# Four PSUM banks in turn for five products by token block, and modulation pieces only in the MLP's second products

## The chip, the cores and the metric

The kernel runs on one core of one Trainium2 chip. The metric is the device time of one launch in microseconds (us). The kernel before takes 2113.64 us, the median of three runs (2110.22 to 2122.06).

The engines are TensorE (PE; PEld is its loading of weights), VectorE (DVE), ScalarE (ACT), GpSimd (POOL) and SyncE (SP), which only issues DMAs here. Each of them works through its own list of instructions in order. PSUM, where PE leaves its products, has eight banks of 128 x 512 floats; DVE and ACT read them and so set them free ("evacuate").

## The reference

512 tokens of 1024 channels, batch 1, go through two blocks, all in float32. The first block has two attention layers, the second a convolution layer and a gated recurrence (hgrn), each of these two followed by an MLP of 4096 hidden channels. A vector `c` per block gives scale, shift and gate of each layer (the "modulation": `silu(c)` times a matrix). What the change touches:

```python
# even mixer: z = h @ w_in, split into
EVEN_SPLITS = [384, 256, 32, 512, 128, 128, 1024]   # cq, ckv, kr, sq, sk, sv, gate
k_rope = apply_rope(z_kr, cos_r, sin_r)             # 32 channels of a token
c_kv = rmsnorm(z_ckv, kv_norm)                      # kv = c_kv @ w_ukv
q = (rmsnorm(z_cq, q_norm) @ w_uq)                  # rope on 32 of each head's 96
q_s = apply_rope(z_sq, cos_h, sin_h)                # sliding window attention
# odd mixer: z = h @ w_in, its first three parts of 512 channels
q, k = apply_rope(z_dq, ...), apply_rope(z_dk, ...)
v_d = z_dv
# MLP of the second block
y = square(relu(h @ w1)) @ w2;  x = x + gate * y    # gate, and the next layer's scale, shift: silu(c) @ ada_w + ada_b
```

## The kernel before

A product in float32 is made of three products of split numbers (a high and a low part, "hTh" and "hTl" for the activations, `hl` for the weights), by `mm3` at L207. Activations stand channel-major, 8 chunks of 128 channels; tokens stand in four blocks of 128. `gemm_x` (`gemm_xs`, L287) computes one product by token block: for each of four blocks it asks for a PSUM bank, issues 24 matmuls (8 chunks x 3 terms) into it, and calls the product's evacuation `evac(tb, ps)`. Weights come in granules of 1024 columns: SP fetches `raw` (4 buffers), ACT casts it to the high part (L221), DVE or POOL makes the low part (L224); `hl` has 5 buffers.

The banks of PSUM are named by tag, `{"mm": 2, "sc": 2, "tp": 2, "pv": 1, "tq": 1}`. A `gemm_x` without `subs` takes the tag `mm`, so its token blocks use two banks in turn; one with `subs` (two parts per block) takes `mm` and `sc` by turns.

In the even mixer these stand one after the other: the product `cq` (L741), the library call `partition_broadcast` on POOL that spreads `nsink` (L745), the product `ckv` of 288 columns (L756; its evacuation takes a sum of squares on ACT, L553, the root on POOL, L386 and L388, a scaling on ACT, L751, and the rope), and the product `sq` of 512 columns (L777; evacuation by rope and a DMA). Then come 20 transposes of the latents (L784, evacuated by ACT, L202, and DVE, L203), the products `uq` and `ukv`, and the gates (L668). `rope` (L575 to L585) reads PSUM twice on DVE (L582 into the scratch tile `ru`, which has one buffer, and L584) and adds on POOL (L585), which sets `ru` free. In the odd mixer three products of 512 columns follow each other: `dq` and `dk` with rope and a DMA issued on ACT (L908), and `dv`, copied by ACT (L938). Before them `nlam` is spread by POOL (L928).

The modulation's vectors are queued (`ada`, L484) in steps: 8 per vector, each fetching 512 KB (`araw`) and adding two scaled rows on DVE (L502 first, then L504) to `acc`, which has one buffer; each fourth step ends a half vector with four small matmuls (L511, PSUM bank `tq` here) and additions (L513, L517). `group()` counts the groups of products (`ng`), and at every `tick_every`-th count `tick()` takes one step from the queue.

The MLP (`mlp`) goes by quarters q = 0 to 3 of its hidden channels. The first product of a quarter is two calls of `gemm_q`, a product of 512 channels in seven parts (L1186, banks `mm`, `sc`, `tp` in turn, sums on DVE at L1179); for q = 0 the first of the two is `gemm_wh` in plain form. `evq` squares the relu and splits it into `hid` (L199 on ACT, L200 on DVE). The second product is two calls of `gemm_x`, whose evacuation (L1100 on DVE, L1103 on POOL) adds to the resident x. Before the MLP of the convolution layer three vectors (24 steps) are queued; with `tick_every` at 2 they came out two per `gemm_q`, two per `gemm_wh` and two per `gemm_x` until the queue was empty.

The instructions of each engine are not in the order of the program: the scheduler takes each instruction with a priority by its place in the program and builds the engines' lists from an estimate of when each would be ready.

Of the kernel before, what the change touches and what calls it, by code (L numbers as in the profile page):

```python
# [26 lines left out]
# layout of the constant array  # L27
# [49 lines left out]
def constants():  # L77
# [16 lines left out]
    # of a row's block of 32: the columns of each level; of a row's block of 128: the block of 32 on the diagonal  # L94
# [13 lines left out]
def cap4(v, o):  # L108
    """512 elements of a DRAM vector as four rows of 128, each on 32 partitions"""
    return bass.AP(tensor=v.tensor, offset=v.offset + o, ap=[[P, 4], [0, 32], [1, P]])  # L110


class K:
# [33 lines left out]
    def scope(self, **bufs):  # L147
        """a pool of working tiles; bufs by tag"""
        @contextmanager
        def f():  # L150
            with self.tc.tile_pool(name=self.nm("wk"), bufs=1, reuse_waits="tile") as p:
                old = (getattr(self, "t4", None), getattr(self, "bufs", None))
                self.t4, self.bufs = p, bufs
                yield p
                self.t4, self.bufs = old
        return f()
# [18 lines left out]
    def oT_tiles(self, t0):  # L175
        """a mixer's output as a split pair: the first token block in t0, the others in the places of the activations
        that the mixer read"""
# [31 lines left out]
    def wgran(self, w, k0, nk, c0, cw, own=False):  # L209
        """weights rows [k0*128, (k0+nk)*128), cols [c0, c0+cw) -> split pair [128, 2, nk, cw]"""  # L210
# [16 lines left out]
    def wload(self, w, c0, cw, kc, own=0):  # L227
        """the weights of kc chunks of channels, the last granules in own tiles of the scope"""
# [9 lines left out]
    def rank(self, off):  # L238
        """instructions that the scheduler takes off places later than their place in the program"""
# [5 lines left out]
    def mark(self):  # L245
        """what comes from the queue of the modulation stays behind the work of DVE so far"""
# [6 lines left out]
    def advance(self, g, have, want):  # L253
        """steps of g until their cost reaches want; the cost so far"""
# [7 lines left out]
    def weave(self, main, n, fill, cost):  # L262
        """n steps of main, with fill of that cost (or of cost(i) after i steps) spread over them, and kept behind
        them on TensorE"""
# [22 lines left out]
    def gemm_xs(self, act, w, c0, cw, kc, evac, tag="mm", subs=None):  # L287
        """out[tok, c0:c0+cw] by token block; evac(tb, psums)"""
        gs = self.wload(w, c0, cw, kc)
        subs = subs or [(0, cw)]  # L290
        for tb in range(NTB):
            outs = []
            for s0, sw in subs:
                ps = self.psum(("mm", "sc")[tb % 2] if len(subs) > 1 else tag)
# [11 lines left out]
    def gemm_xk(self, act, gs, cw, kc, evac):  # L306
        """as gemm_x, with the channels outermost"""
# [9 lines left out]
    def gemm_tb(self, act, w, evac, after=None, late=None):  # L317
        """out[tok, 0:1024], a token block's two halves one after the other; evac(tb, half, psum). with late,
        the last channels come late: the first half of two token blocks does the others first, the second block after
        that instruction"""  # L320
# [29 lines left out]
    def gemm_ws(self, act, w, c0, cw, kc, evac, tag="mm"):  # L350
        """out[c0:c0+cw, tok] by chunks of 128 channels; evac(chunk, psum)"""
# [14 lines left out]
    def gemm_wh(self, act, jobs):  # L366
        """as gemm_w for jobs (w, c0, evac) of 256 channels, the first half of the tokens before the second"""
# [14 lines left out]
    def rstd(self, ss, n, cols=1):  # L382
        """(ss/n + eps)^-1/2"""
# [8 lines left out]
    def cond(self, cs):  # L392
        """silu of each vector of cs, as columns [128, 8]"""
# [10 lines left out]
    def start(self, x_in, c, c2, w, b, g, wg, cw):  # L404
        """norm and modulation of the first layer: the normalised x channel-major while the modulation's weights
        come in; returns silu(c) and the step that makes chunk k of the split pair"""
# [77 lines left out]
    def ada(self, ccol, w, b, c0, kind, g=None):  # L484
        """one vector of the modulation as a row in DRAM, queued in eight steps"""
# [50 lines left out]
    def group(self):  # L536
        """after each group of products of a weight"""
# [18 lines left out]
    def prenorm(self, act, tb, x, S, B, eng=None):  # L556
        """rmsnorm and modulation of token block tb [128 tok, 1024], to its columns of the split channel-major pair"""
# [15 lines left out]
    def rope(self, out, src, tb, nh, dim, co, so):  # L573
        """out, src [128, nh, dim] views; src in PSUM or SBUF"""
# [13 lines left out]
    def softmax(self, ps, n, mask, sink=None, norm=True):  # L588
        """ps holds minus the scores; returns the probabilities [128, n]"""
# [19 lines left out]
    def heads_T(self, src, n, sel, scale=None, tag="b4"):  # L609
        """src [128 tok, NTB, x]; sel(src, tb) -> [128, n]; transposed, split pair tile [128, 2, 512]"""  # L610
# [10 lines left out]
    def p_T(self, p, nb):  # L621
        """p [128 q, nb*128 keys] -> [128 keys, nb, 128 q]"""
# [8 lines left out]
    def pv32(self, out, V, p, qb):  # L631
        """out[:, qb] = sum over the key blocks V of V^T p^T, in float32"""
# [6 lines left out]
    def pv_pair(self, out, Vs, ps, qb):  # L639
        """the same for two heads of 64 channels, on the two halves of the columns of the array"""  # L640
# [8 lines left out]
    def pv_out(self, o, pv):  # L649
        """o = pv * o / 2, o holding twice the silu of the gate"""  # L650
# [11 lines left out]
    def gates(self, act, w, c0, o, cs):  # L662
        """o[c] = 2 silu(gate), with silu(x) = x (1 + tanh(x/2)) / 2"""
# [7 lines left out]
    def vec_cols(self):  # L671
        """per-channel vectors as columns: [128, 54]"""
# [20 lines left out]
    def out_first(self, o, w, xsrc, xdst, GG, S, B):  # L693
        """o: [128, 8, 512] fp32; returns the next split activations"""
# [1093 lines left out]
```

## Time and profile before

| what | value |
|---|---|
| median of three runs | 2113.64 us |
| span of the profiled execution | 2106.4 us |
| PE busy | 1943.9 us, 92% of the span |
| DVE busy | 1402.8 us, 67% |
| ACT busy, POOL busy | 884.5 us, 805.1 us |
| TensorE's mean granted clock | 0.959 of full |

The profile is of one execution, and its span runs from its first to its last instruction; the median of the runs is 7.2 us above it. The rows further below come from the page of that execution and from its trace. Times are from the start of the span. In a row of the timeline the first number is the start and the second the length in us (of xN instructions together), and the bracket at the end is how long the engine had waited and what ended the wait.

### The profile page before, as it was taken

What the parts mean: (1) busy time and instruction counts of PE and PEld (TensorE: products, weight loads), DVE (VectorE), ACT (ScalarE), POOL (GpSimd) and SP (SyncE); (2) the same over time, 40 slices, a digit from 0 to 9 for tenths busy, and PEclk for the clock granted to TensorE, in tenths of its full rate; (3) what the DMA queues carried; (4) which work ended last, traced back from release to release, by engine and by line L of the source; (5) the groups of instructions that cost most, each with busy time, mean ns of one, the idle gap of its engine ahead of it and who ended that gap; (6) DMA issues with size and microseconds to landing.
All of it is one profiled execution on the core that took longest, in us unless ns stands there. A gap on an engine that the chain in (4) does not pass through costs nothing.

```text
span 2106.4 us, 32096 instructions
## 1 busy us (share of the span) xinstructions
PE 1943.9 (92%) x12471; PEld 1580.0 (75%) x12471; DVE 1402.8 (67%) x1987; ACT 884.5 (42%) x1499; POOL 805.1 (38%) x701
## 2 busy tenths in 40 slices
PE   7799999897999988679899999999999998999998
PEld 5688667664776776448788989876777778898896
DVE  5356775545555769976987648667787858485673
ACT  4245553134544434333525436243454534352452
POOL 1223334222233448615232422455585544223232
PEclk9899979998999999889999999999999999999999
DMA  8384555366343751432554235453322322242331
GB/s 317 121 230 142 173 165 157 88 156 144 87 129 94 250 165 56 110 105 91 170 187 132 83 99 178 132 151 106 101 78 87 116 86 80 90 131 71 121 101 60
DMA packets 225024, 270.67 MB, mean 128 GB/s; under 512 B 26602, under 2 KB 145609, under 8 KB 224872
## 3 DMA queue, kind: packets, MB, share of 16 engines
q1 hardware_dynamic: 188982, 232.83, 36.3%
q10 hardware_dynamic: 35890, 35.79, 5.5%
q8 instruction: 98, 1.61, 0.3%
q14 instruction: 54, 0.44, 0.1%
HBM read 252.46 MB, written 16.12 MB: 128 GB/s over the span
## 4 chain that ended last, share of the span: by engine, by line
PE 49%; DVE 14%; issue 6%; DMA 6%; POOL 4%; ACT 2%; ACTq 0%; POOLq 0%; DVEq 0%; SPq 0%
PE mm L207 28%; PE sc L207 5%; PE mm L1186 4%; PE sc L1186 3%; PE tp L1186 3%; DVE acc L504 3%; DMA araw<-in_ada_w_dram 2%; DVE hl L224 2%; DVE ol L1312 2%; DVE hl L200 1%; DMA raw<-in_od_w_in_dram 1%; DVE X L1547 1%; PE pv L207 1%; DMA raw<-in_ada_w_dram 1%; PE tp L626 1%
## 5 line engine op out<-in xcount | busy, mean ns | idle before, releaser
L207 PE MATMUL mm<-hTh,hl 128*128 128x512 f32 (+1 forms) x1296 | 410.9, 393 | 19.0 <-ACT t L1339 7.0
L207 PE MATMUL mm<-hl,hid 128*128 128x512 f32 x1344 | 317.0, 395 | 5.3 <-DVE hid L200 3.8
L221 ACT CAST hl<-raw 128x1024 fp32r<-128x1024 f32 (+2 forms) x219 | 224.1, 1033 | 223.8 <-PE mm L207 133.8
L207 PEld LDWEIGHTS mm<-hl,hid 128*128 128x128 f32 x1344 | 251.9, 188 | 65.2 <-DVE hid L200 4.9
L207 PEld LDWEIGHTS mm<-hTh,hl 128*128 128x128 f32 x1296 | 242.8, 194 | 74.6 <-ACT t L1339 7.9
L224 DVE TENSOR_TENSOR hl<-raw,hl 128x1024 fp32r<-128x1024 f32 (+2 forms) x186 | 251.3, 1361 | 67.3 <-ACT hl L221 66.8
L207 PE MATMUL mm<-hTl,hl 128*128 128x512 f32 (+2 forms) x648 | 253.2, 391 | 0.9 <-DVE hTl L200 0.8
L207 PE MATMUL mm<-hl,hTh 128*128 128x512 f32 (+3 forms) x752 | 220.5, 371 | 26.9 <-DVE t L584 11.9
L1103 POOL TENSOR_TENSOR xr<-xr,t 128x512 f32<-128x512 f32 x56 | 80.4, 1435 | 303.4 <-DVE t L1100 303.4
L504 DVE SCALAR_TENSOR_TENSOR acc<-araw,ccol,acc 128x512 f32<-128x512 f32 x182 | 158.5, 871 | 45.0 <-DMA araw<-in_ada_w_dram 31.4
L207 PEld LDWEIGHTS mm<-hl,hTh 128*128 128x128 f32 x752 | 140.0, 197 | 52.2 <-ACT t L751 9.6
L603 POOL TENSOR_TENSOR s<-s,sm 128x256 f32<-128x256 f32 (+3 forms) x112 | 82.7, 739 | 184.0 <-DVE sm L599 165.4
L207 PEld LDWEIGHTS mm<-hTl,hl 128*128 128x128 f32 (+1 forms) x648 | 125.6, 194 | 26.4 <-DVE hTl L200 1.5
L199 ACT CAST hl<-raw 128x1024 fp32r<-128x1024 f32 x84 | 86.8, 1048 | 136.1 <-PE mm L207 111.3
L200 DVE TENSOR_TENSOR hl<-raw,hl 128x1024 fp32r<-128x1024 f32 x84 | 131.3, 1578 | 13.5 <-ACT hl L199 12.9
L207 PE MATMUL mm<-hl,hTl 128*128 128x512 f32 (+3 forms) x376 | 138.8, 369 | 0.3 <-DVE hTl L457 0.3
L224 POOL TENSOR_TENSOR hl<-raw,hl 128x1024 fp32r<-128x1024 f32 x33 | 84.3, 2554 | 131.5 <-ACT hl L221 131.4
L1166 POOL TENSOR_TENSOR raw<-raw,raw 128x1024 f32<-128x1024 f32 x28 | 76.2, 2722 | 147.1 <-DVE rows L1166 85.2
L1100 DVE TENSOR_TENSOR t<-mm,rows 128x512 f32<-128x512 f32 x56 | 38.5, 687 | 104.3 <-PE mm L207 104.0
L598 ACT ACTIVATE s<-s,sm 128x256 f32<-128x256 f32 (+5 forms) x128 | 69.6, 544 | 90.7 <-DVE sm L596 86.7
L1312 DVE SCALAR_TENSOR_TENSOR ol<-u,dw,ol 128x512 f32<-128x512 f32 x90 | 103.2, 1147 | 2.9
L207 PE MATMUL sc<-b,b 64*128 64x256 f32 (+7 forms) x384 | 92.2, 356 | 12.5 <-DVE sm L596 11.7
(358 smaller groups left out, 3956.4 us busy)
## 6 DMA issues: line engine op xcount, KB each, us to landing
raw<-in_mlp_w_dram SPq DMA_DIRECT2D x128, 512.0 KB
araw<-in_ada_w_dram SPq DMA_DIRECT2D x72, 512.0 KB
raw<-in_hgrn_w_in_dram SPq DMA_DIRECT2D x40, 512.0 KB
araw<-in_w_ada_dram SPq DMA_DIRECT2D x32, 512.0 KB
raw<-in_od_w_in_dram SPq DMA_DIRECT2D x32, 512.0 KB
raw<-in_ada_w_dram SPq DMA_DIRECT2D x24, 512.0 KB
rows<-row SPq DMA_DIRECT2D x16, 512.0 KB
raw<-in_conv_w_in_dram SPq DMA_DIRECT2D x16, 512.0 KB
```

Of the source, the lines that this page charges most:

```text
L199: nc.scalar.copy(out=hi, in_=src)
L200: nc.vector.tensor_tensor(out=lo, in0=src, in1=hi.bitcast(F32), op=ALU.subtract)
L207: self.nc.tensor.matmul(out, lhsT=lt[a], rhs=rt[b], start=start and n == 0, stop=stop and n == 2)
L221: self.nc.scalar.copy(out=hi, in_=raw[:, :n])
L224: eng.tensor_tensor(out=lo, in0=raw[:, :n], in1=hi.bitcast(F32), op=ALU.subtract)
L504: eng.scalar_tensor_tensor(out=acc, in0=raw[:, k], scalar=c, in1=acc, op0=ALU.mult, op1=ALU.add)
L598: nc.scalar.activation(out=s[:, :m], in_=s[:, :m], func=AF.Exp, scale=-1.0, bias=mn, accum_out=sm)
L603: nc.gpsimd.tensor_tensor(out=p, in0=p, in1=r.to_broadcast([P, n]), op=ALU.mult)
L1103: eng.tensor_tensor(out=xs, in0=xs, in1=t, op=ALU.add)
L1166: eng.tensor_tensor(out=out, in0=x, in1=y, op=f)
L1186: nc.tensor.matmul(ps[:, m * 256:m * 256 + 256], lhsT=ws[n][:, a, k, m * P:m * P + P], rhs=parts[n][b][:, k], start=m + k + t == 0, stop=m ...
L1312: nc.vector.scalar_tensor_tensor(out=yc, in0=u[:, j:j + T], scalar=dw[:, cc, j:j + 1], in1=yc, op0=ALU.mult, op1=ALU.add)
```

## The change

`gemm_xs` knows a tag `wide`, with which its token blocks take the banks `mm`, `sc`, `mm`, `sc`. The products `ckv` and `sq` of the even mixer and the three products of the odd mixer have it. In `gemm_q` the four calls of `group()` are gone, and while `gemm_wh` runs in `mlp` the interval is set to 1000, so that the queue is served by the MLP's second products alone: by program order 8 steps in each of those of q = 0, 1 and 2. The MLP of the hgrn layer has an empty queue. Comments and docstrings are taken out as well.

```diff
@@ gemm_xs
-                ps = self.psum(("mm", "sc")[tb % 2] if len(subs) > 1 else tag)
+                ps = self.psum(("mm", "sc")[tb % 2] if len(subs) > 1 or tag == "wide" else tag)
@@ even
-        self.gemm_x(act, w, 384, 288, KC, ev_ckv)
+        self.gemm_x(act, w, 384, 288, KC, ev_ckv, tag="wide")
...
-            self.gemm_x(act, w, 672, 512, KC, ev_sq)
+            self.gemm_x(act, w, 672, 512, KC, ev_sq, tag="wide")
@@ odd
-        self.gemm_x(act, w, 0, 512, KC, ev_rope(0))
-        self.gemm_x(act, w, 512, 512, KC, ev_rope(1))
+        self.gemm_x(act, w, 0, 512, KC, ev_rope(0), tag="wide")
+        self.gemm_x(act, w, 512, 512, KC, ev_rope(1), tag="wide")
...
-        self.gemm_x(act, w, 1024, 512, KC, ev_vd)
+        self.gemm_x(act, w, 1024, 512, KC, ev_vd, tag="wide")
@@ gemm_q
         out(0, 0, c11)
-        self.group()
...
         out(1, 0, c21)
-        self.group()
...
         out(1, 1, u3)
-        self.group()
         add(u2, u2, prod(6))
         out(0, 1, u2)
-        self.group()
@@ mlp
                 next(parts)
+                hold, self.tick_every = self.tick_every, 1000
                 self.gemm_wh(act, [(w1, m * 256, lambda c, ps, m=m: ev(2 * m + c, ps)) for m in range(2)])
+                self.tick_every = hold
                 parts = next(parts)
```

The first place at which the engines' lists move is DVE's list at the end of the even mixer's product `sq`. `mm_775`, `mm_806`, `mm_837`, `mm_868` are the banks of its four token blocks, `mm_958` is that of the first `uq` block, `hl_950` to `hl_1093` are weights of `uq` and `ukv`, and `b_151` to `b_155` the transposed latents. Before:

```order
L582 TENSOR_TENSOR ru_801<-mm_775,cst 128x512
L584 TENSOR_TENSOR t_140_800<-mm_775,cst 128x512
L203 SCALAR_TENSOR_TENSOR b_154_902<-tp_925,vcols,b_154_902 128x512
L203 SCALAR_TENSOR_TENSOR b_155_903<-tp_932,vcols,b_155_903 128x512
L582 TENSOR_TENSOR ru_832<-mm_806,cst 128x512
L584 TENSOR_TENSOR t_143_831<-mm_806,cst 128x512
L582 TENSOR_TENSOR ru_863<-mm_837,cst 128x512
L584 TENSOR_TENSOR t_146_862<-mm_837,cst 128x512
L224 TENSOR_TENSOR hl_950<-raw_948,hl_950 128x768
L224 TENSOR_TENSOR hl_955<-raw_953,hl_955 128x768
L224 TENSOR_TENSOR hl_1088<-raw_1086,hl_1088 128x1024
L582 TENSOR_TENSOR ru_894<-mm_868,cst 128x512
```

The same place in the changed kernel:

```order
L582 TENSOR_TENSOR ru_801<-mm_775,cst 128x512
L224 TENSOR_TENSOR hl_950<-raw_948,hl_950 128x768
L224 TENSOR_TENSOR hl_955<-raw_953,hl_955 128x768
L224 TENSOR_TENSOR hl_1088<-raw_1086,hl_1088 128x1024
L224 TENSOR_TENSOR hl_1093<-raw_1091,hl_1093 128x1024
L203 SCALAR_TENSOR_TENSOR b_151_899<-tp_904,vcols,b_151_899 128x512
L203 SCALAR_TENSOR_TENSOR b_152_900<-tp_911,vcols,b_152_900 128x512
L203 SCALAR_TENSOR_TENSOR b_153_901<-tp_918,vcols,b_153_901 128x512
L203 SCALAR_TENSOR_TENSOR b_154_902<-tp_925,vcols,b_154_902 128x512
L584 TENSOR_TENSOR t_140_800<-mm_775,cst 128x512
L203 SCALAR_TENSOR_TENSOR b_155_903<-tp_932,vcols,b_155_903 128x512
L582 TENSOR_TENSOR ru_832<-sc_806,cst 128x512
```

Four evacuations of `sq`, which stood between its products, now stand behind the weights' low parts and all five latents; PE's 20 transposes have moved behind the whole product as well.

The second place is ACT's list in the odd mixer's second product (`dk`), whose weights are `hl_3910` to `hl_3925`; `t_914` to `t_940` are the roped blocks that L908 sends to DRAM after POOL's L585, and `hl_4077` is the first granule of `dv`. Before:

```order
L908 DMA dqk<-t_914_3800 128x512
L923 ACTIVATE sm_3744<-sm_3744 1x2
L948 DMA sm_4245<-in_od_forget_bias_dram 8x1
L908 DMA dqk<-t_917_3831 128x512
L221 CAST hl_3915<-raw_3913 128x1024
L221 CAST hl_3920<-raw_3918 128x1024
L908 DMA dqk<-t_922_3867 128x512
L221 CAST hl_3925<-raw_3923 128x1024
L221 CAST hl_4077<-raw_4075 128x1024
```

The same place in the changed kernel:

```order
L908 DMA dqk<-t_914_3800 128x512
L923 ACTIVATE sm_3744<-sm_3744 1x2
L948 DMA sm_4245<-in_od_forget_bias_dram 8x1
L221 CAST hl_3915<-raw_3913 128x1024
L221 CAST hl_3920<-raw_3918 128x1024
L221 CAST hl_3925<-raw_3923 128x1024
L908 DMA dqk<-t_917_3831 128x512
L221 CAST hl_4077<-raw_4075 128x1024
L908 DMA dqk<-t_922_3867 128x512
```

The last weight of `dk` no longer stands behind the DMA of a block that POOL has yet to finish.

The third place is DVE's list in the convolution layer's MLP, in the second `gemm_q` of q = 2, a quarter without pieces before. `t_2131` to `t_2155` are the sums of the seven parts and their activations' source, `hl_10647` to `hl_10829` weights. Before:

```order
L1179 TENSOR_TENSOR t_2155_10610<-t_2154_10609,sc_10637 128x512
L200 TENSOR_TENSOR hid_10511<-t_2132_10373,hid_10511 128x2x256
L200 TENSOR_TENSOR hl_10606<-raw_10577,hl_10606 128x1024
L200 TENSOR_TENSOR hid_10454<-t_2132_10373,hid_10454 128x2x256
L1179 TENSOR_TENSOR t_2154_10609<-t_2154_10609,tp_10663 128x512
L224 TENSOR_TENSOR hl_10814<-raw_10812,hl_10814 128x1024
L1179 TENSOR_TENSOR t_2155_10610<-t_2155_10610,mm_10694 128x512
L224 TENSOR_TENSOR hl_10819<-raw_10817,hl_10819 128x1024
L200 TENSOR_TENSOR hid_10691<-t_2154_10609,hid_10691 128x2x256
L1179 TENSOR_TENSOR t_2154_10609<-t_2155_10610,sc_10720 128x512
```

The same stretch in the changed kernel, in which `acc_10963` is the sixth half vector and the tiles have other numbers (`t_2154_10609` is `t_2140_10551` here, `hid_10454` is `hid_10396`):

```order
L1179 TENSOR_TENSOR t_2141_10552<-t_2140_10551,sc_10579 128x512
L504 SCALAR_TENSOR_TENSOR acc_10963<-araw_10996,ccol_93,acc_10963 128x512
L200 TENSOR_TENSOR hl_10548<-raw_10519,hl_10548 128x1024
L200 TENSOR_TENSOR hid_10396<-t_2118_10315,hid_10396 128x2x256
L1179 TENSOR_TENSOR t_2140_10551<-t_2140_10551,tp_10605 128x512
L224 TENSOR_TENSOR hl_10756<-raw_10754,hl_10756 128x1024
L504 SCALAR_TENSOR_TENSOR acc_10963<-araw_10996,ccol_93,acc_10963 128x512
L1179 TENSOR_TENSOR t_2141_10552<-t_2141_10552,mm_10636 128x512
L224 TENSOR_TENSOR hl_10761<-raw_10759,hl_10761 128x1024
L504 SCALAR_TENSOR_TENSOR acc_10963<-araw_11028,ccol_93,acc_10963 128x512
L224 TENSOR_TENSOR hl_10766<-raw_10764,hl_10766 128x1024
L1179 TENSOR_TENSOR t_2140_10551<-t_2141_10552,sc_10662 128x512
```

The scheduler has drawn the steps of the second products forward. Of the six half vectors, one stood in `gemm_wh`, one in the `gemm_q` of q = 0, two in the second product of q = 0 and two in the first product of q = 1. In the changed kernel one stands in `gemm_wh`, one at the turn to the second product of q = 0, and two each in the first products of q = 1 and q = 2.

## Rows read from the trace of the kernel before

**Rows 1.** The page, its head and the busy time of the engines.

```profile
span 2106.4 us, 32096 instructions
...
PE 1943.9 (92%) x12471; PEld 1580.0 (75%) x12471; DVE 1402.8 (67%) x1987; ACT 884.5 (42%) x1499; POOL 805.1 (38%) x701
```

**Rows 2.** Timeline of PE in the even mixer.

```profile
75.36 0.58 PE L207 MATMUL mm<-hl,hTh 128*128 128x288 f32 x1 [9.34 <-DVE t L584]
```

**Rows 3.** Windows at half clock: stretch, length, busy time by engine, PEclk, DMA share, GB/s.

```profile
68.00:78.30 10.30, 2.94 (x12) 2.96 (x13) 1.23 (x4) 2.47 (x6) 1.77 (x5) 0.50 0.09 14
...
388.90:399.10 10.20, 6.27 (x14) 4.49 (x15) 4.85 (x6) 1.99 (x2) 3.57 (x3) 0.50 0.35 103
```

**Rows 4.** Timeline of POOL in the even mixer.

```profile
65.95 0.28 POOL L745 PARTITION_BROADCAST nsink<-sm  x1 [6.28 <-issue]
73.53 0.18 POOL L386 TENSOR_SCALAR sm<-sm 128x1 f32<-128x1 f32 x1 [7.29 <-issue]
...
92.20 1.30 POOL L585 TENSOR_TENSOR t<-t,ru 128x512 f32<-128x512 f32 x1 [4.13 <-DVE t L584]
```

**Rows 5.** Timeline of DVE in the even mixer, from the product sq on.

```profile
90.78 0.69 DVE L582 TENSOR_TENSOR ru<-mm,cst 128x512 f32<-128x512 f32 x1 [3.04 <-PE tp L784]
91.39 0.68 DVE L584 TENSOR_TENSOR t<-mm,cst 128x512 f32<-128x512 f32 x1
91.98 1.40 DVE L203 SCALAR_TENSOR_TENSOR b<-tp,vcols,b 128x512 fp32r<-128x512 f32 x2
96.75 0.69 DVE L582 TENSOR_TENSOR ru<-mm,cst 128x512 f32<-128x512 f32 x1 [3.37 <-PE mm L207]
...
102.32 0.69 DVE L582 TENSOR_TENSOR ru<-mm,cst 128x512 f32<-128x512 f32 x1 [4.28 <-PE mm L207]
...
104.71 1.15 DVE L224 TENSOR_TENSOR hl<-raw,hl 128x768 fp32r<-128x768 f32 x1 [1.10 <-ACT hl L221]
...
108.86 0.68 DVE L582 TENSOR_TENSOR ru<-mm,cst 128x512 f32<-128x512 f32 x1
...
121.51 0.28 DVE L584 TENSOR_TENSOR t<-sc,cst 128x128 f32<-128x128 f32 x1
```

**Rows 6.** Timeline of PE in the odd mixer's first three products.

```profile
368.85 1.23 PE L568 MATMUL tp<-cst,t 128*128 128x128 f32 x8 [2.02 <-DVE t L565]
370.65 0.47 PE L207 MATMUL mm<-hl,hTh 128*128 128x512 f32 x1 [0.57 <-DVE t L584]
...
392.79 0.79 PE L207 MATMUL mm<-hl,hTh 128*128 128x512 f32 x1 [6.57 <-ACT hl L221]
...
416.58 0.47 PE L207 MATMUL mm<-hl,hTh 128*128 128x512 f32 x1 [1.94 <-DVE t L584]
```

**Rows 7.** Timeline of POOL in the odd mixer.

```profile
382.76 0.28 POOL L928 PARTITION_BROADCAST nlam<-sm  x1 [5.87 <-issue]
389.97 1.25 POOL L585 TENSOR_TENSOR t<-t,ru 128x512 f32<-128x512 f32 x1 [6.93 <-issue]
```

**Rows 8.** Timeline of ACT in the odd mixer (ACTq is its DMA issue).

```profile
391.25 0.33 ACTq L908 DMA_DIRECT2D dqk<-t  x1
391.69 1.99 ACT L221 CAST hl<-raw 128x1024 fp32r<-128x1024 f32 x2 [11.32 <-POOL t L585]
```

**Rows 9.** Windows of the convolution layer's MLP: PE, PEld, DVE, ACT, POOL busy, PEclk, DMA share, GB/s.

```profile
983.60:1036.80 53.20, 47.76 (x378) 46.47 (x376) 51.53 (x50) 24.89 (x34) 17.61 (x8) 0.94 0.38 124
1036.80:1085.90 49.10, 46.58 (x209) 36.21 (x209) 38.66 (x46) 14.42 (x19) 16.12 (x9) 1.00 0.56 179
1085.90:1133.10 47.20, 43.84 (x354) 42.90 (x353) 45.31 (x53) 23.83 (x31) 13.77 (x4) 0.93 0.60 192
...
1179.70:1219.70 40.00, 40.00 (x338) 40.00 (x337) 36.04 (x36) 24.68 (x34) 10.60 (x4) 1.00 0.41 133
```

**Rows 10.** Waits of PE from 983.6 to 1133.1: us in total, times, longest.

```profile
PE tq L511 <- DVE acc L504: 3.4, 1, 3.4
PE mm L207 <- DVE hid L200: 2.5, 2, 1.7
```

## The prediction

> **What bounds the kernel now.** I read the page's head first: PE is busy 92% of the span and DVE 67% [rows 1], so most of the kernel goes at PE's pace, and a change gains only where PE stands still or runs at its lower clock. Then I went through PE's timeline for waits of over 1 us, looked up in the timelines of DVE, POOL and ACT what ended each, and took windows around them. In the places that the change touches there are three kinds.
>
> The even mixer has one of 9.3 us, ended by DVE's L584 [rows 2], which is the reading of a PSUM bank. It came late because POOL was away: 6.28 us before the broadcast of `nsink` and 7.29 us before the next root are "issue" [rows 4], in which it waited for nothing that the trace shows; the root is what the evacuation of `ckv` begins with. Both `mm` banks were full, so PE stood. Until 78.3 it then ran at a granted clock of 0.50, which is 1.2 of 2.4 GHz [rows 3].
>
> The odd mixer has the same outage of POOL, 5.87 and 6.93 us around the broadcast of `nlam` [rows 7]. Here PE waits 6.57 us, not for a bank but for ACT's cast of a weight [rows 6], and ACT had stood 11.32 us until POOL's L585 [rows 8]: the cast of `hl_3925` stands behind the DMA of a block that POOL had not finished. With it go 10.2 us at a clock of 0.50, and two smaller waits, 2.02 and 0.57 us before the products and 1.94 us at 416.6 [rows 3, 6].
>
> The MLP of the convolution layer has waits for DVE: 3.4 us for `acc` in the first product of q = 1, and 2.5 us at the second product of q = 0 [rows 10]. The first products of q = 1 take 47.2 us with pieces of modulation, those of q = 2 without them 40.0 us, with PE busy all the time [rows 9].
>
> **The even mixer.** Nothing is added in instructions; five products write other banks. Blocks three and four of `ckv` no longer wait, so PE does them inside the 9.3 us hole. The next product, `sq`, then needs the first `ckv` bank, whose release is the very event that ended the hole at 75.4 [rows 2]. Its four blocks take 5.57 us each, the distance of two evacuations (96.75 to 102.32) [rows 5], 22.3 us in all. With 2.4 us on top, an estimate for a half clock after the wait that is left (10.3 us at 0.50 followed the hole before [rows 3]) and for the last weights, which are split late, it ends at about 100.1; before, its last evacuation began at 108.9 [rows 5], so PE is 8 to 9 us earlier.
>
> The gain is given back behind it. Before, three of the four `sq` evacuations stood between its blocks on DVE, at 90.8, 96.8 and 102.3. Now the order puts four low parts of weights and four of the five L203 of the latents in front of the second half of the first evacuation, and `uq` needs those same four banks. From 100.1 on DVE does: four L224 at some 1.15 us, of which one is done by then (3.5); four L203 at 0.70 (2.8); the rest of the first evacuation, L584 and POOL's L585, 0.68 + 1.30 (2.0); three more, each 0.69 + 0.68 + 1.30, because `ru` has one buffer (8.0) [rows 4, 5]; then the eight evacuations of `uq`. Before, these ran from 112.45 (3.6 us after the start of the last `sq` evacuation) to 121.8, about 9.1 us. The sum is 25.4, so `uq` is done at about 125.5 instead of 121.8 [rows 5]: 3 us later, rounded. The cheapest case is that the low parts and the L203 are ready early and cover POOL's 1.30 us: then 6 to 8 us of the gain stay. The dearest is that everything is in series and PE, waiting 2.7 us before each part of `uq`, falls to half clock: +17 and more. I take +3, since it is the sum of the order's rows with durations from the trace.
>
> **The odd mixer.** By the order, the cast of `hl_3925` stands ahead of both DMAs that wait for POOL, so the 6.57 us go. The half clock behind them goes too: in the 10.2 us at 0.50 PE was busy 6.27 us [rows 3], half of which, 3.1, is the loss. The first block of the third `dq` bank (`mm_3842`) now goes ahead of the last transposes and fills 2.02 + 0.57 us, and `dv` no longer waits 1.94 us for a bank [rows 6]. That makes 14.2 us. What is late next: POOL still returns at about 390 [rows 7], and every roped block costs 2.67 us of DVE and POOL in a row. The eighth block (`sc_4025`) needs the bank that is set free by the first evacuation after the return, at about 392.6, and reaches it at about 395; `dv`'s second weight is cast behind the DMA of the sixth block, at about 400, for a product that begins at about 401. Both hold by 1 to 2 us, so I take off 1 us: -13, between -4.5 (only the bank waits go, 2.59 + 1.94) and -15.
>
> **The MLP.** The change says that the pieces come only in second products; the order of the changed kernel says otherwise, since the scheduler draws their DVE work forward into first products. The count of six half vectors is unchanged; they move later. Two of them in a first product cost DVE 45.3 - 36.0 = 9.3 us [rows 9]. In q = 0, DVE is busy 51.5 of 53.2 us of the first product; it loses one half vector but then stands waiting for L511 behind the last of the seven parts, and the sums for the second product queue behind that, so the waits of 2.5 us stay in size: -1. The second product of q = 0 loses one of two half vectors: -1. In q = 1 the wait of 3.4 us for `acc` goes, since `tq_10109` stands one product later than its sums need; DVE's 45.3 us become the bound instead of 47.2: -2. In q = 2 DVE goes from 36.0 to 45.3 us beside 40.0 us of PE [rows 9]: between 0, if its surplus is worked off in the second product, and +7.2, if it goes as in q = 1 before; I take the middle, +3. The sum is -1, between -8 and +8.
>
> **Sum.** +3 - 13 - 1 = -11 us, against the profiled span of 2106.4 us: 2095.4, or 0.9948 of it. The median of the runs is 7.2 us above the span; 0.9948 of 2113.64 is 2103 us. What a measurement of this kernel can tell from no change is about 0.5%, 10.6 us, so the forecast lies on that border.
>
> **Rivals.**
> First, the even mixer gains as well: DVE's list at `sq` runs without holes because weights and latents are ready early. For it speaks that DVE is free 3 to 4 us before each `sq` evacuation [rows 5]; against it, that the four low parts need slots that the last `sq` block sets free. -8 - 13 - 1 = -22: 2092.
>
> Second, the odd mixer's wait only changes its name: PE runs ahead by the banks and meets the same weights. For it speaks that a weight and not a bank ended the longest wait there [rows 6, 8], against it that the cast has moved in ACT's list. Then 4.5 us are saved: +3 - 4.5 - 1 = -2.5: 2111.
>
> Third, DVE becomes the bound in q = 2 as it was in q = 1: +7.2 there instead of +3, with its lag carried into the second product: -7 or less: 2107.
>
> Fourth, slower: the evacuations of `sq`, moved behind the product, hold every part of `uq` for 2.7 us, and PE falls to 1.2 GHz for `uq` and what follows. PE's work from 108.9 to 121.8 is some 13 us at most and `ukv` is estimated at as much again; at half speed that adds up to 26 us to the 3 of lateness, +29 - 13 - 1 = +15: 2128. It decides from some 20 us of PE's work at 0.50 on. For it speaks the 10 us at 0.50 behind each long wait [rows 3], against it that the first matmul behind the waits of 0.57 and 1.94 us takes 0.47 us, and only the one behind 6.57 us takes 0.79 [rows 6].
>
> Fifth, taking banks in turn is itself what costs: if the clock fell to 0.50 for it, the twenty blocks of the five products, about 5.57 us each, would take up to twice as long; five blocks are enough for +28 - 13 = +15 or so, 2128 and up. Against it: the first product of q = 2 takes `mm`, `sc` and `tp` in turn and has a granted clock of 1.00 throughout its 40 us [rows 9]. The Trainium skill has this as a rule, in "TensorE: Matmul & The Clock Gate", section "A second HAM failure mode: psum-queue depth-cycling": going round PSUM banks with each iteration leaves small gaps in PE's work, and the clock swings between half and full. By that rule this change would lose; the rows of q = 2 do not agree with it here.
>
> **Chances.** The forecast 0.44 (its own range 2096 to 2111; of it 0.26 under the border of 0.5% and 0.18 over it), the first rival 0.18, the second 0.16, the third 0.10, the fourth 0.10 (0.02 of it within 0.5%), the fifth 0.02. That is 0.44 for faster by over 0.5%, 0.46 for within 0.5% and 0.10 for slower. The range for 8 of 10 goes from the first rival's time less 4 to the second's plus 7: 2088 to 2118; the fourth and fifth, 0.12, are mostly left out.
>
> **What would show it.** Right: PE without the 9.3 us wait near 66 to 75, but with waits of 1 to 3 us at L207 on `uq`, ended by DVE's L584, from about 100 on; PE without a wait over 2 us from 368 to 410, and the third odd product some 13 us earlier against the first; no wait for `acc` at L511 in q = 1; DVE at over 44 us in the first product of q = 2. Wrong: a cast L221 that still ends a wait of over 4 us in the odd mixer, a granted clock of 0.50 from 100 to 130, a first product of q = 2 of over 46 us, or one of under 41 us together with an even mixer that ends earlier than before.

## The result, and the profile after

The changed kernel takes 2124.44 us (median of nine runs, 2116.23 to 2136.72), the kernel before 2113.14 us in the nine runs beside it. The ratio is 1.0054, with a 95% interval of 1.0032 to 1.0076: the change makes the kernel 11 us slower. The forecast of 2103 us was wrong, in sign and beyond its range.

The profiled execution of the changed kernel was the slowest of its nine (2136.72 us); that of before, with a span of 2106.4 us, stands at the fast end of its own. So a difference between the two traces is read below for its place and its mechanism, and its size is taken from the timed runs of kernels that carry one part of the change. This is the head of the page after, to set beside [rows 1]:

```profile
span 2134.9 us, 32085 instructions
...
PE 1970.3 (92%) x12471; PEld 1596.8 (75%) x12471; DVE 1404.1 (66%) x1987; ACT 885.5 (41%) x1499; POOL 799.5 (37%) x701
```

PE takes 26 us more of busy time for the same number of matmuls, while DVE, ACT and POOL changed by less than 1%. With that goes a lower clock of TensorE: its mean is 0.946 instead of 0.959.

Six marks in PE's timeline, the same instructions in both kernels, show where the difference arises (us; in brackets how much later than before):

| mark on PE | before | after |
|---|---|---|
| `ckv` starts (waits for L736) | 57.0 | 57.8 (+0.8) |
| a wait at the start of the even attention (L599) | 154.5 | 160.5 (+5.9) |
| out projection of the even layer starts | 308.4 | 326.4 (+18.0) |
| wait for the gates of the odd layer (L668) | 460.1 | 472.6 (+12.5) |
| first part of the seven in the convolution layer's MLP to wait | 1011.5 | 1029.9 (+18.3) |
| first wait in hgrn (L1547, L1545 after) | 1458.6 | 1483.1 (+24.5) |

**The even products** end 5 us late, counted from the start of `ckv`. The 9.3 us wait of [rows 2] is a 3.7 us wait now, but the evacuations of `sq` are late. DVE's timeline after, to set beside [rows 5]:

```profile
87.39 0.69 DVE L582 TENSOR_TENSOR ru<-mm,cst 128x512 f32<-128x512 f32 x1 [0.42 <-POOL t L585]
98.86 0.96 DVE L224 TENSOR_TENSOR hl<-raw,hl 128x768 fp32r<-128x768 f32 x1 [10.78 <-ACT hl L221]
...
107.95 0.69 DVE L584 TENSOR_TENSOR t<-mm,cst 128x512 f32<-128x512 f32 x1
...
110.03 0.69 DVE L582 TENSOR_TENSOR ru<-sc,cst 128x512 f32<-128x512 f32 x1
...
112.75 0.69 DVE L582 TENSOR_TENSOR ru<-mm,cst 128x512 f32<-128x512 f32 x1 [1.44 <-POOL t L585]
...
127.44 0.28 DVE L584 TENSOR_TENSOR t<-sc,cst 128x128 f32<-128x128 f32 x1
```

Between the two readings of the first `sq` bank lie 20.6 us. For 10.8 of them DVE stood, since the next instruction of its list was a weight's low part, which waited for ACT's cast. The last evacuation of `uq` ends at 127.7 instead of 121.8. From 107 to 113, over the last transposes and the first blocks of `uq`, TensorE's granted clock was 0.50 (it was 1.00 from 100 to 130 before):

```profile
107.00:113.00 6.00, 5.33 (x17) 4.97 (x18) 3.89 (x7) 0.93 (x2) 2.55 (x2) 0.50 0.46 132
```

**The even attention**, 930 matmuls from the second mark to the third in both kernels, takes 165.9 us instead of 153.9. Windows of before, first the whole stretch and then its tail:

```profile
154.50:308.40 153.90, 150.05 (x930) 110.33 (x930) 109.33 (x307) 79.58 (x226) 55.83 (x100) 0.89 0.52 158
279.10:308.40 29.30, 28.59 (x124) 17.97 (x124) 19.23 (x56) 12.70 (x42) 10.40 (x22) 0.53 0.55 170
```

The same of after, its tail first:

```profile
290.95:326.30 35.35, 32.52 (x127) 19.80 (x127) 19.61 (x58) 13.27 (x45) 10.66 (x24) 0.50 0.50 147
...
160.50:326.35 165.85, 158.60 (x930) 114.67 (x930) 110.67 (x306) 79.75 (x226) 55.82 (x100) 0.83 0.51 148
```

The tail, short matmuls behind the last gate products, runs at a granted clock of about 0.5 in both (0.53 and 0.50); the whole stretch has a mean of 0.83 instead of 0.89.

**The odd layer.** PE has no wait over 1 us in its three products. But at the gates behind them it waits more than twice as long as before (4.24 us then). PE before, PE after, and ACT after:

```profile
460.06 0.50 PE L207 MATMUL mm<-hTh,hl 128*128 128x512 f32 x1 [4.24 <-DVE o L668]
```

```profile
472.57 0.80 PE L207 MATMUL mm<-hTh,hl 128*128 128x512 f32 x1 [9.75 <-DVE o L668]
```

```profile
463.05 1.04 ACT L221 CAST hl<-raw 128x1024 fp32r<-128x1024 f32 x1 [10.66 <-DMA raw<-in_od_w_in_dram]
...
471.20 0.60 ACT L667 ACTIVATE o<-mm 128x512 f32<-128x512 f32 x1
```

ACT waits for the DMA of a weight, and the gate's L667 stands behind that cast.

**The MLP.** Windows after, first and second products of q = 0, 1, 2 by turns (of the first product of q = 0 only the second call, `gemm_q`):

```profile
1025.50:1054.80 29.30, 23.19 (x179) 22.44 (x177) 28.93 (x27) 15.04 (x18) 6.42 (x3) 0.88 0.52 162
1054.80:1102.80 48.00, 46.51 (x205) 36.09 (x201) 26.50 (x35) 15.90 (x21) 15.21 (x10) 1.00 0.36 113
1102.80:1148.10 45.30, 42.43 (x345) 41.78 (x345) 43.99 (x49) 23.80 (x32) 9.70 (x4) 0.96 0.53 173
1148.10:1195.30 47.20, 45.87 (x202) 36.13 (x200) 23.08 (x27) 13.99 (x18) 15.19 (x10) 1.00 0.31 107
1195.30:1241.70 46.40, 42.22 (x345) 41.53 (x345) 44.33 (x48) 24.04 (x32) 9.35 (x4) 0.96 0.54 175
1241.70:1288.60 46.90, 45.88 (x203) 36.15 (x201) 22.78 (x27) 13.70 (x18) 15.24 (x10) 1.00 0.24 77
```

Beside [rows 9]: the first product of q = 2 takes 46.4 us instead of 40.0, its second product 46.9 instead of 44.7 (before):

```profile
1219.50:1264.20 44.70, 44.70 (x195) 36.25 (x194) 18.23 (x22) 12.44 (x15) 14.80 (x10) 1.00 0.22 71
```

Of these 2.2 us, 1.0 is a wait of PE for DVE's L200; the rest is PE's own work (busy 45.9 us instead of 44.7), with the eight matmuls of a half vector (L511) that were not there before.

### The profile page after: what moved, and what is told of

It is laid out like the page before. It is cut to its first block, busy times and chain, and to the rows that moved or that the text cites. A ratio compares the mean times of both kernels' runs of the same rounds, so it can differ in the third digit from the quotient of the medians.

```text
span 2134.9 us, 32085 instructions
## 1 busy us (share of the span) xinstructions
PE 1970.3 (92%) x12471; PEld 1596.8 (75%) x12471; DVE 1404.1 (66%) x1987; ACT 885.5 (41%) x1499; POOL 799.5 (37%) x701
## 4 chain that ended last, share of the span: by engine, by line
PE 46%; DVE 15%; DMA 6%; issue 6%; POOL 4%; ACT 2%; SPq 0%; ACTq 0%; POOLq 0%; DVEq 0%
PE mm L207 27%; PE sc L207 5%; PE mm L1186 3%; DVE acc L504 3%; PE sc L1186 3%; PE tp L1186 2%; DMA araw<-in_ada_w_dram 2%; DVE hl L224 2%; DVE ol L1310 2%; DVE hl L200 1%; DMA raw<-in_ada_w_dram 1%; DVE X L1545 1%; PE pv L207 1%; PE tp L626 1%; DVE acc L502 1%
## 5 line engine op out<-in xcount | busy, mean ns | idle before, releaser
L207 PEld LDWEIGHTS mm<-hTh,hl 128*128 128x128 f32 x1296 | 245.4, 196 | 81.2 <-DVE o L668 10.2
L207 PE MATMUL mm<-hl,hTh 128*128 128x512 f32 (+3 forms) x592 | 173.1, 369 | 12.7 <-ACT t L736 4.4
L200 DVE TENSOR_TENSOR hl<-raw,hl 128x1024 fp32r<-128x1024 f32 x84 | 127.8, 1533 | 15.7 <-ACT hl L199 14.9
L207 PEld LDWEIGHTS mm<-hl,hTh 128*128 128x128 f32 x592 | 110.4, 199 | 31.1 <-ACT t L736 4.7
L1166 POOL TENSOR_TENSOR raw<-raw,raw 128x1024 f32<-128x1024 f32 x28 | 71.9, 2567 | 153.2 <-DVE rows L1166 103.3
L207 PE MATMUL mm<-hl,hTl 128*128 128x512 f32 (+3 forms) x296 | 108.7, 367 | 0.6 <-DVE hTl L457 0.6
L207 PE MATMUL sc<-b,b 64*128 64x256 f32 (+7 forms) x384 | 98.5, 370 | 10.9 <-DVE sm L596 8.7
```

What stands on the lines that cost most here:

```text
L200: nc.vector.tensor_tensor(out=lo, in0=src, in1=hi.bitcast(F32), op=ALU.subtract)
L207: self.nc.tensor.matmul(out, lhsT=lt[a], rhs=rt[b], start=start and n == 0, stop=stop and n == 2)
L1166: eng.tensor_tensor(out=out, in0=x, in1=y, op=f)
```

## The experiments

**One part each.** e1_odd, e2_even and e3_mlp carry the odd products, the even products and the MLP's part of the change alone; e6_ckv carries only the product `ckv`.

```diff
 # e1_odd: gemm_xs as changed, and the three products of odd
+        self.gemm_x(act, w, 0, 512, KC, ev_rope(0), tag="wide")
 # e2_even: gemm_xs, and the two products of even;  e6_ckv: the first of them
+        self.gemm_x(act, w, 384, 288, KC, ev_ckv, tag="wide")
+        self.gemm_x(act, w, 672, 512, KC, ev_sq, tag="wide")
 # e3_mlp: gemm_q without group(), the interval of 1000 around gemm_wh
```

> Only the three products of the odd mixer take four banks in turn; all else as before. Theory A (the loss lies in the even mixer and the MLP, the odd products gain and give half back at the gates behind them): the stretch from the end of the out projection (308 us in the profile of before) to the first gate's wait (460 us) gets about 5.5 us shorter, the wait for DVE's L668 there grows from 4.2 to some 9 us, and the time falls by 4 to 8 us, ratio 0.996 to 0.998. Rival B (what the changed kernel's odd stretch shows depends on what came before it): the whole 13 us are gained, ratio 0.994 or less.

> Only the two products of the even mixer take four banks. Theory A (moving these evacuations changes the order of the attention behind them, and PE loses its clock there): slower by 12 to 18 us, ratio 1.006 to 1.009, with more than 10 us of the difference between 160 and 326 us and over 45 us at a granted clock of 0.50 in the even attention, where before has 34. Rival B (the profiled execution of the changed kernel was a slow one in its clock, and the products cost only what was late at uq): slower by 3 to 6 us, ratio 1.001 to 1.003, and the attention as long as before.

> Only the MLP's pieces move; all banks as before. Theory A (DVE is the bound in the first products of q = 1 and q = 2): slower by 2 to 6 us, ratio 1.001 to 1.003, the first product of q = 2 at 45 us instead of 40 and that of q = 1 no shorter than 46. Rival B (the wait of 3.4 us for acc is all that counts): faster by 1 to 4 us, ratio 0.998 to 0.9995.

> Only the product ckv takes four banks. Theory A (it is the evacuations of sq, queued behind weights and latents, that make uq late): the 9.3 us wait goes, sq starts some 8 us earlier and its evacuations stay between its blocks: the end of uq is 4 to 8 us earlier than before; with an attention in another order the time is 0 to 6 us below before, ratio 0.997 to 1.000. Rival B (any change of the order ahead of the attention costs clock in it): the time is 5 us or more above before in spite of the earlier start, ratio 1.0025 or more.

Measured: e1_odd 0.9983 (0.9966 to 1.0000), e2_even 1.0048 (1.0028 to 1.0068), e3_mlp 1.0026 (1.0006 to 1.0045), e6_ckv 1.0014 (0.9996 to 1.0033). The first three add up to 1.0057, the change as a whole is 1.0054, so within these intervals the parts simply add up: -3.6, +10 and +5.5 us of some 2112. The time of e3_mlp is in theory A's range, though its first products of q = 1 and q = 2 take 45.1 and 42.8 us, less than the 46 and 45 of A. e1_odd lies just above A's range, and its interval reaches 1; in its trace the stretch is 7.1 us shorter and the wait 9.9 us, as in A. e2_even lies between, with a ratio below that of A and above that of B. Its trace has 4.1 us more than before from `ckv` to the attention's first wait and 6.0 us more from there to the out projection, with 37.5 us at 0.50 that begin in the tail and end in the out projection, where before has 27.3. e6_ckv is near theory A in the products (they end 3.7 us earlier against `ckv`'s start; A had 4 to 8) and neither in the time; the attention behind it is 3.6 us longer in its trace.

**Why sq is evacuated late.** e5_even_tr is e2_even with the transposes of the latents ahead of `sq` in the program; e13_tr has that move alone; e12_t4 is e2_even with six `t4` tiles.

```diff
 # e5_even_tr (with wide), e13_tr (without): the block moves up
+        cT = [self.b4() for _ in range(5)]
+        for c in range(5): ...   # 20 transposes and their evacuation
         o = self.otile()
...
             self.gemm_x(act, w, 672, 512, KC, ev_sq, tag="wide")
-        cT = [self.b4() for _ in range(5)]
-        for c in range(5): ...
 # e12_t4
-..., h["ev_w_out"][0], t4=4, ru=1, ...
+..., h["ev_w_out"][0], t4=6, ru=1, ...
```

> As e2_even (the even mixer's two products on four banks), but the transposes of the latents (L784) stand ahead of the product sq in the program. Theory A (the evacuations of sq were late because each needs a t4 tile, all four of which the latents hold until they are transposed; with four banks PE no longer stops before sq, so the transposes came behind it): the evacuations of sq stand between its blocks again, the first attention transposes (the wait at 154.5 us before, 160.2 in e2_even) start at 146 to 152 us, and the time is 5 us or more below that of e2_even, ratio 1.003 or less. Rival B (DVE and POOL are too slow for sq in any case): that wait stays at 157 us or later and the ratio at 1.004 or more.

> As e2_even, with six t4 tiles in the even mixer instead of four, and the transposes where they were. Theory A (the t4 tiles alone held up the evacuations of sq): those evacuations come at intervals of 5 to 6 us between the blocks of sq, the wait that e2_even has at 160.2 us comes at 156 or before, and the time is at least 5 us below that of e2_even, ratio 0.997 to 1.0025. Rival B (the transposes behind sq cost as much by themselves, since PE then has nothing else to do while the latents are evacuated): that wait stays at 158 us or later and the ratio at 1.0035 or more.

> The transposes ahead of sq alone, all products on two banks as before. Theory A (the gain of e5_even_tr comes from the four banks, and the transposes only clear their way): no change, ratio 0.9985 to 1.0015, the wait of 9.3 us on ckv still there. Rival B (the order of the transposes is the gain, whatever the banks): ratio 0.997 to 0.9985 here too.

Measured: e5_even_tr 0.9985 (0.9968 to 1.0001), e12_t4 1.0030 (1.0012 to 1.0048), e13_tr 0.9989 (0.9969 to 1.0009). DVE's first `sq` evacuations in e5_even_tr (L775 is the transposes' line there), and then in e12_t4:

```profile
90.01 0.69 DVE L582 TENSOR_TENSOR ru<-mm,cst 128x512 f32<-128x512 f32 x1 [0.36 <-POOL t L585]
96.19 0.69 DVE L584 TENSOR_TENSOR t<-mm,cst 128x512 f32<-128x512 f32 x1 [3.48 <-PE tp L775]
98.28 0.69 DVE L582 TENSOR_TENSOR ru<-sc,cst 128x512 f32<-128x512 f32 x1 [0.29 <-POOL t L585]
```

```profile
87.15 0.69 DVE L582 TENSOR_TENSOR ru<-mm,cst 128x512 f32<-128x512 f32 x1 [0.36 <-POOL t L585]
87.75 0.68 DVE L584 TENSOR_TENSOR t<-mm,cst 128x512 f32<-128x512 f32 x1
90.87 0.69 DVE L582 TENSOR_TENSOR ru<-sc,cst 128x512 f32<-128x512 f32 x1 [2.43 <-PE sc L207]
...
96.44 0.69 DVE L582 TENSOR_TENSOR ru<-mm,cst 128x512 f32<-128x512 f32 x1 [4.28 <-PE mm L207]
```

The bracket of 96.19 names the cause: the second reading of the bank waits for PE's transposes. It writes a `t4` tile, the even mixer has four, and the four latents hold them all until they are transposed. With two banks PE stopped before `sq`, and the transposes went into that hole; with four it does not stop there as long, and they came behind `sq`. With two more tiles the two readings follow each other at once, and the evacuations come at the pace of PE.

From the start of `ckv` to the attention's first wait it takes 97.6 us before, 101.6 in e2_even, 98.0 in e12_t4, 94.2 in e5_even_tr and 100.4 in e13_tr, where the wait of 9.3 us on `ckv` is 10.8 us long. So the tiles' theory holds for the evacuations. But the tiles give back only half of what the earlier transposes do: in e12_t4 the latents still stand behind `sq`, and DVE waits for them (3.2 us at 111.4, for ACT's L202), which is part of rival B. The four banks are worth 3.4 us there against before, and 6.2 against e13_tr, whose profiled execution was the slowest of its twelve. The times follow less clearly: e5_even_tr is 0.63% faster than e2_even, but its interval and that of e13_tr overlap almost wholly, so no time shows what the banks add to the transposes' place. e12_t4 lies above the range of its theory A, and the interval of e13_tr holds both of its theories. The attention's first wait comes at 153.3 us in e5_even_tr, a little later than its theory A has it.

What is left is the attention. In the profiled executions its 930 matmuls take 153.8 us before, 159.8 in e2_even, 158.3 in e12_t4, 157.4 in e6_ckv, 155.4 in e13_tr and 151.4 in e5_even_tr. By their traces PE works through it in the same order in before, e13_tr, e5_even_tr, e11_all and the kernels of the odd mixer and the MLP (151.4 to 155.4 us in all of them). Only e6_ckv, e12_t4 and e2_even have other orders, and the changed kernel has that of e2_even. So the other orders go with 4 to 6 us more than before, and the further 6 us of the changed kernel come with the lower clock of its profiled execution (0.83, against 0.88 in e2_even). Most of what the orders add lies in the tail: 127 matmuls in 32.2 to 34.6 us in these three, 124 in 27.1 to 30.2 us with the order of before. The tail of e2_even:

```profile
285.40:320.00 34.60, 31.00 (x127) 18.82 (x127) 19.50 (x58) 13.18 (x45) 11.38 (x24) 0.54 0.51 151
```

Which feature of the order makes it longer wasn't tried and stays open.

**Why the odd layer keeps only a part of its gain.** e8_odd_hold is e1_odd with modulation held back from the product `dv` to the third gate; e9_hold has that alone.

```diff
         self.gemm_x(act, w, 512, 512, KC, ev_rope(1), tag="wide")
+        hold, self.tick_every = self.tick_every, 1000
...
-            yield from self.gates(act, w, 3080, o, range(6))
+            yield from self.gates(act, w, 3080, o, range(3))
+            self.tick_every = hold
+            self.mark()
+            yield from self.gates(act, w, 3080, o, range(3, 6))
```

> As e1_odd, but no modulation step is queued from the product dv to the third gate, and those behind it wait for DVE's work up to there. Theory A (the products' gain of 12 us was halved because the weights of the fourth gate are fetched behind two pieces of modulation in SP's queue, which wait for acc): the wait for L668 falls from 9.9 us to 3 to 6 us and comes 4 to 6 us earlier than in e1_odd, at 448 to 450 us; ratio 0.994 to 0.997. Rival B (something else, the rope's evacuations or the copies of dv, holds the gates): that wait stays at 452 us or later, ratio 0.998 or more.

> The holding back of modulation steps of e8_odd_hold alone, with all banks as before. Theory A: the gates' wait of 4.2 us becomes under 1 us, as the weights come earlier; at most 4 us faster, ratio 0.998 to 1.000. Rival B (the steps cost where they come instead): slower by 2 to 5 us, ratio 1.001 to 1.0025.

Measured: e8_odd_hold 0.9974 (0.9957 to 0.9991), e9_hold 1.0009 (0.9993 to 1.0026). SP, ACT and PE in e1_odd:

```profile
430.30 1.95 SPq L497 DMA_DIRECT2D araw<-in_ada_w_dram  x2
432.30 29.59 SPq L213 DMA_DIRECT2D raw<-in_od_w_in_dram  x7
```

```profile
444.51 1.04 ACT L221 CAST hl<-raw 128x1024 fp32r<-128x1024 f32 x1 [10.84 <-DMA raw<-in_od_w_in_dram]
```

```profile
454.04 0.80 PE L207 MATMUL mm<-hTh,hl 128*128 128x512 f32 x1 [9.93 <-DVE o L668]
```

PE and ACT in e8_odd_hold:

```profile
453.30 0.50 PE L207 MATMUL mm<-hTh,hl 128*128 128x512 f32 x1 [3.95 <-DVE o L668]
```

```profile
443.76 1.05 ACT L221 CAST hl<-raw 128x1024 fp32r<-128x1024 f32 x1 [4.85 <-DMA raw<-in_od_w_in_dram]
```

In e1_odd the last `dv` block is copied at 427.5 us, 12 us earlier than before; the products do gain what was forecast. But the gates' weights (L213) stand in SP's queue behind two pieces of modulation (L497), which wait 3.3 and 1.1 us for DVE's `acc`, and they only move up by 6 us. Without those pieces the wait for L668 falls from 9.9 to 3.95 us, the size that theory A gives. From the start of the out projection to the end of that wait it takes 151.7 us before, 144.6 in e1_odd and 140.9 in e8_odd_hold, so the gates come 3.7 us earlier; the other 2.3 us of the shorter wait are PE's products, which end that much later in e8_odd_hold.

The place, 453.3 us, is that of rival B, though in an execution whose out projection began 2.9 us later than in e1_odd, and the ratio lies between the two theories. So the traces show the mechanism, and the times do not separate e8_odd_hold from e1_odd. Nor is the gates' wait the whole loss: from there to the MLP the trace of e1_odd takes 554.1 us and that of before 547.1, where the kernels with two banks in the odd products have 543.4 to 550.7; what that stretch adds was not followed. e9_hold leaves the wait at 4.3 us and the time where it was. Its interval reaches into both of its theories, but the wait did not become shorter as A has it; ACT's casts ahead of the gates' weights wait for PE's products there, which end no earlier.

**Where the MLP's pieces belong.** e10_mlp_mark is e3_mlp with a mark at each second product, behind which its pieces stay on DVE.

```diff
             if q < 3:
+                self.mark()
                 for n in range(2):
                     self.gemm_x([L(0), L(1)], w2[q * 1024:(q + 1) * 1024, :], n * 512, 512, KC, mk(n))
```

> As e3_mlp, but each second product of the MLP sets a mark, so that the pieces queued in it come after DVE's work up to there: the pieces then stand in the second products alone on DVE, two half vectors in each of q = 0, 1, 2. Theory A (in e3_mlp the scheduler had drawn them into the first products, where DVE was the bound): first products of q = 1 and q = 2 at 40 to 41 us (e3_mlp 45.1 and 42.8, before 47.1 and 39.8), second products at most 49, and the time 3 to 8 us below before, ratio 0.996 to 0.9985. Rival B (DVE is full in the second products too once they carry the pieces): second products of q = 1 and q = 2 at 50 us or more, ratio 1.000 or above.

Measured: 0.9957 (0.9940 to 0.9973), 9 us faster than before, a little more than theory A has it, where e3_mlp is 5.5 us slower. Windows of e10_mlp_mark, in the order of those above:

```profile
1007.50:1034.60 27.10, 22.15 (x169) 21.95 (x169) 26.96 (x25) 18.89 (x25) 6.05 (x2) 0.87 0.38 119
1034.60:1080.20 45.60, 45.60 (x210) 36.25 (x208) 35.87 (x39) 12.05 (x16) 16.02 (x10) 1.00 0.53 163
1080.20:1120.70 40.50, 40.32 (x341) 40.08 (x338) 35.01 (x36) 23.40 (x33) 10.21 (x4) 1.00 0.40 129
1120.70:1166.80 46.10, 46.10 (x210) 36.23 (x208) 36.78 (x40) 13.49 (x17) 16.35 (x10) 1.00 0.55 165
1166.80:1206.80 40.00, 40.00 (x340) 39.98 (x338) 35.93 (x37) 24.46 (x34) 10.19 (x4) 1.00 0.45 135
1206.80:1253.00 46.20, 46.20 (x211) 36.27 (x209) 35.63 (x38) 12.45 (x16) 16.43 (x10) 1.00 0.46 138
```

With the pieces in the second products DVE is busy some 36 us in each product but the first, and from the second on PE hardly waits. The six together take 245.5 us, 263.1 in the changed kernel and 257.1 before.

**All of it, with the three clearances.** e11_all is the changed kernel with the edits of e5_even_tr, e8_odd_hold and e10_mlp_mark.

> The changed kernel's five products on four banks and its MLP, with the three clearances: transposes ahead of sq, modulation held back behind the third gate of the odd mixer, and a mark at each second product of the MLP. If the three add up as their ratios (0.9985, 0.9974, 0.9957), 0.992: 2094 us. If they collide (each frees time that the next one also frees, or the modulation held back meets the MLP's), 0.995 or above.

Measured: 2083.25 us, 0.9865 (0.9838 to 0.9892): 28 us faster than before, more than the three ratios make together. It beats both kernels. Its parts were not taken out one by one, so the cause of the surplus is open. Its trace shows the place of the gain: 4 us from `ckv` to the attention, 11.7 in the odd mixer up to the gates' wait and 9.5 from the MLP to hgrn. The odd mixer's part is there in the trace of e8_odd_hold too (10.8 us), of which the time keeps 5.5.

## Why the prediction was wrong, point by point

- **Even mixer, +3.** Up to `uq` the term held: 4.1 us in e2_even. The step "three more, each 0.69 + 0.68 + 1.30" read DVE's list rightly; that the list had this form because of the `t4` tiles I had not seen, though `t4` of the even mixer stands in the call. Two readings were off without harm to the sum: the 10.3 us at 0.50 lie over the hole, with only 2.9 of them behind it [rows 2, 3], and the evacuations of `uq` before took 9.35 us, not 9.1. The waits of 1 to 3 us on `uq` did not come (0.9 us at most); PE waited 2.3 us for DVE's L203 at the transposes instead. The term failed by where it ends: I added nothing for the attention behind, whose order changes too and which takes 6.0 us more in e2_even; its time is 10 us longer, not 3.
- **Odd mixer, -13.** The failing step is "What is late next": I followed the weights and banks of `dk` and `dv` and stopped at the end of `dv`. There the gain was 12 us. The next weights of the gates hung on DVE's `acc` through SP's queue, and not only on PE's progress: the gates' wait grew from 4.2 to 9.9 us. The time kept -3.6 us (-7 to 0).
- **The MLP, -1.** That the scheduler draws the pieces forward was right, and so was the end of the wait for `acc` (0.3 us after, 3.4 before [rows 10]). The term for q = 2, "I take the middle, +3", was +6.4 in the changed kernel, at a granted clock of 0.96, and +2.8 in e3_mlp, at 1.00. The sum held nothing for the second product behind it, which takes 2.2 us more (46.9 instead of 44.7) and 3.4 more in e3_mlp. In the six windows e3_mlp is 3.4 us longer than before, not 1 shorter.
- **The rivals.** The third, DVE as the bound in q = 2, happened, though not alone. The fourth had the right place, the even mixer, but the wrong price: in the changed kernel the clock was at 0.50 over the beginning of `uq` alone (107 to 113 above), not over the 26 us of work that the rival counted. The fifth did not happen: e5_even_tr and e11_all take four banks in turn and are no slower than before. The second was wrong in the products and right one stage later, where the wait for a weight did return.
- **The sum.** Three terms of -13, +3 and -1 measured -3.6, +10 and +5.5. The runs put most of the error into what comes behind the edited products: the attention, the gates' weights and the second product of q = 2. The largest term, -13, was off by 9 us.

## What to carry to other kernels

When a product is given more banks, look up what its evacuations write into: a free bank gains nothing while a neighbour holds the tiles of that pool. A gain must be followed to the next weights of the stage behind, through the queue that fetches them and whatever stands ahead of them there. Where a scheduler orders the work, "only in this product" is true of the program alone, and a mark that ties the pieces to it was worth 0.69%, some 14.5 us, here (e10_mlp_mark against e3_mlp, each by its ratio to before).

## What the runs showed of the hardware

At one place the same matmuls in the same order ran at either level of TensorE's clock, and the level went with the length of the wait ahead of them. The order of e3_mlp is that of before up to the MLP. One wait in the odd attention, PE for DVE's L200, is 0.87 us in the profiled execution of before and 2.14 us in that of e3_mlp. The 10.2 us behind it, in before and in e3_mlp:

```profile
588.90:599.10 10.20, 10.20 (x52) 8.01 (x53) 7.53 (x22) 4.84 (x13) 2.11 (x4) 1.00 0.47 157
```

```profile
594.10:604.30 10.20, 10.20 (x31) 7.81 (x31) 6.73 (x17) 4.29 (x10) 1.83 (x3) 0.50 0.51 157
```

52 matmuls at 2.4 GHz stand against 31 at 1.2 GHz. Six more kernels have PE's matmuls around this place in the same order: behind waits of 0.65 us (e10_mlp_mark) and 1.41 us (e5_even_tr) the 10.2 us hold 52 matmuls at 1.00; behind 1.73 us (e1_odd), 1.76 (after), 1.83 (e13_tr) and 1.93 (e6_ckv) they hold 38 or 39 at a mean of 0.67. So executions differ by several us in a stretch that no edit touched, and a single pair of traces does not give the size of a change of 0.5%.
